# A layer step with attention, scan and ConvFFN: three value units moved between the convolved groups, two z groups behind them

## The chip, the cores and the metric

The kernel runs on one core of a Trainium2 chip. Its time is that of one execution on the device, in microseconds; what is given is the median of several executions, and beside it one execution with the hardware profiler on, from which all rows below are. TensorE does the matmuls, VectorE and GpSimd the elementwise work, ScalarE activations and copies, and SyncE's queue issues the DMAs.

## The reference

One layer on 512 prompt tokens and 32 sample tokens, with shared weights. What the change touches is the first part:

```python
h = rmsnorm(x, g_mix)
q, k, v, z, xbc, dt_raw, gates = jnp.split(h @ w_in, split_at, axis=-1)
q, k = rmsnorm(q, g_q), rmsnorm(k, g_k)             # by head
ya = band_attention(q, k, v, rel_bias)              # cached_attention for the sample tokens
xbc_c = silu(causal_dwconv(xbc, conv_ssm_w, conv_ssm_b))
xs, bm, cm = jnp.split(xbc_c, ...)                  # 32 heads, 4 groups of B and C
y, h_fin = ssd(xs, dt, a_log, bm, cm, h0)           # chunked scan
yb = rmsnorm((y + d_skip * xs) * silu(z), g_ssm)
x = x + (gate_a * (ya @ w_proj_a) + gate_b * (yb @ w_proj_b)) @ w_out
```

Then follow the ConvFFN and a gated addition. New k and v rows, the scan's state and the convolutions' last columns are outputs too.

## The kernel before, in words

All 544 tokens lie in the free dimension, features in the partitions. The large matmuls are a stream of steps (`dense_steps`, line 38), each of which makes 128 output features: 8 chunks of 6 matmuls (`mm3`, line 273: the weight as a high and a low part, the activations too, three products, two halves of 272 tokens). A step here is called a unit. The weight tile of a unit is loaded by DMA in the order of the stream, two units in one load; ScalarE rounds it to the high part (line 250), and the rest (line 254) is made by VectorE, for odd units below 40 by GpSimd. That happens one unit ahead.

A unit ends with its epilogue, which reads the two PSUM banks of `dps` (two such buffers):

- xbc units (`ep_xbc`, line 580) are the convolved ones, six to a group `proj(g)`: B, C and four x. VectorE scales them into `ext` (lines 571, 573, 574), ScalarE does the first tap (596), VectorE three more (599), ScalarE tanh (602), VectorE the product (603, 604). GpSimd copies a few columns.
- z units (`ep_z`, line 714): one VectorE scaling (717), tanh on ScalarE, two VectorE products (720, 721), a square and a sum on ScalarE and GpSimd. Four z units need the finished scan of their group.
- q and k units (`ep_qk`, line 734): scaling, square and split; nine chunks later `qk_norm` (line 745) does two small sums on TensorE, Ln and Exp on ScalarE and a product on VectorE.
- v units (`ep_v`, line 761): one VectorE scaling (763), the output DMA (764), and three chunks later five transposes on TensorE with two ScalarE copies (`v_transpose`, line 767).

TensorE's order is the order of the program's text: every matmul and transpose is pinned behind the one before (`Ordered`, line 122). Between chunks, the text from line 1136 on places other work by counts of chunks: from chunk 70 the scan, sixteen pairs of `ssd_a` (line 613) and `ssd_b` (line 664), a group of four every 65 chunks, up to chunk 330; then attention. `ssd_b` of a group's first pair, which holds stage 4 (sample tokens) and stage 0, comes at chunks 97, 162, 227 and 292. It runs the yps matmuls, adds them to xs on VectorE (line 690), and runs the st matmuls (line 696). The small PSUM tiles, `cbt`, `xst`, `yps`, `st`, `vt`, `vs`, `qn`, `cum` and others, share four banks (`sps`, line 172). `dt_sums` (line 519) comes at chunk 56.

On VectorE, ScalarE, GpSimd and SyncE the order of instructions is chosen by a list scheduler at build time, from the text's order and estimated times.

Before `do_logexp` (line 728) ScalarE's table is set for tanh and exp; `do_logexp` sets the one for Ln and Exp when the first q unit and the fourth pair's q unit come (line 1153).

Of the kernel before, what the change touches and what calls it, by code (L numbers as in the profile page):

```python
# [37 lines left out]
def dense_steps():  # L38
    def proj(g):
        return [("xbc", "B", g), ("xbc", "C", g)] + [("xbc", "x", i) for i in range(4 * g, 4 * g + 4)]  # L40

    def z(g):
        return [("z", i) for i in range(4 * g, 4 * g + 4)]

    def qkv(m):
        return [("qk", m, 0), ("qk", m, 1), ("v", m)]

    p = proj(0)
    p += proj(1) + proj(2) + z(0) + proj(3) + z(1)
    for m in range(NPAIR):  # L50
        p += qkv(m)
        if m == 2:
            p += z(2)
    p += z(3)
    p += [("ga", m) for m in range(8)]
    p += [("pa", m) for m in range(8)] + [("gb", m) for m in range(8)]
    p += [("pb", m) for m in range(8)] + [("out", m) for m in range(8)]

    def up(t):
        return [(n, i) for i in range(8 * t, 8 * t + 8) for n in ("ug", "uv")]  # L60

    def down(t):
        return [("down", t, m) for m in range(8)]

    p += up(0) + up(1) + down(0) + up(2) + down(1) + down(2)
    p += [("pw", m) for m in range(8)] + [("gate", m) for m in range(8)]
    return p
# [35 lines left out]
def unit_order():  # L103
    return [u for st in dense_steps() for u in units_of(st)]
# [12 lines left out]
def trunk(ctx: ExitStack, tc: tile.TileContext, a):  # L117
# [170 lines left out]
    class Dense:  # L288
        def __init__(self):
            self.steps = dense_steps()  # L290
            self.i = 0
            self.count = 0
            self.cur = None
            self.later = []
# [987 lines left out]
```

## Time and profile before

| | |
|---|---|
| median of 3 executions | 1355.56 us (1354.17 to 1358.21) |
| the profiled execution | 1355.77 us |
| its span, first to last instruction | 1354.1 us |
| TensorE (PE) busy | 1338.2 us |
| VectorE (DVE) busy | 852.6 us |
| ScalarE (ACT) busy | 634.4 us |
| GpSimd (POOL) busy | 313.7 us |
| TensorE's granted clock | 0.999 |

A row of instructions names the line of the kernel, the engine, the operation, the tiles written and read, and shapes; times are microseconds from the first instruction unless they are marked as ns. Idle time of an engine before an instruction is put down to what released it.

### The profile page before, as it was taken

The page shows a single profiled execution, that of the slowest core. Times are in us where ns is not written, and L with a number is a line of the kernel's source. Part 1 is how long each engine was busy: PE and PEld are TensorE (multiplying, and loading weights), DVE is VectorE, ACT ScalarE, POOL GpSimd, SP SyncE. Part 2 cuts the span into 40 slices and gives each one's busy share as a digit, 9 for nine tenths or more (in the row PEclk, how much of TensorE's full clock was granted, in tenths as well). Part 3 has the DMA queues.
Part 4 walks back from the last instruction along what each step waited for, and adds up shares of the span by engine and source line. Part 5 has one row for each costly group of instructions (what it writes and reads, how often), then busy time and mean ns, then how long its engine had stood idle before and what let it go on. Part 6 is the DMA issues. An engine that isn't in the chain of part 4 may idle for free.

```text
span 1354.1 us, 26563 instructions
## 1 busy us (share of the span) xinstructions
PE 1338.2 (99%) x11045; PEld 1307.2 (97%) x11045; DVE 852.6 (63%) x1474; ACT 634.4 (47%) x1104; POOL 313.7 (23%) x442
## 2 busy tenths in 40 slices
PE   8999999999999999999999999999999999999998
PEld 7999998999999999999999999999999999999998
DVE  7999889755775656643554335677676356753545
ACT  5465555656676667542442223534444124432342
POOL 5456365544321211100000000133332013310000
PEclk9999999999999999999999999999999999999999
DMA  5733243332533332222223422222222232222231
GB/s 182 252 100 130 83 128 121 119 132 100 177 94 114 115 111 90 67 81 94 69 89 110 143 94 73 85 94 94 94 72 85 94 111 94 76 85 94 94 107 53
DMA packets 41896, 142.15 MB, mean 105 GB/s; under 512 B 9216, under 2 KB 13232, under 8 KB 29488
## 3 DMA queue, kind: packets, MB, share of 16 engines
q1 hardware_dynamic: 41776, 140.45, 31.4%
q8 instruction: 87, 1.43, 0.4%
q14 instruction: 33, 0.27, 0.1%
HBM read 129.27 MB, written 14.31 MB: 106 GB/s over the span
## 4 chain that ended last, share of the span: by engine, by line
PE 89%; DVE 6%; ACT 2%; DMA 1%; issue 1%; SPq 0%; POOL 0%; ACTq 0%; DVEq 0%; POOLq 0%
PE dps L130 80%; PE O L130 2%; PE yps L130 2%; PE L L130 1%; PE st L130 1%; DVE cv L599 1%; DVE qs L834 1%; PE Tp L133 1%; DVE wl L254 1%; PE xst L133 0%; PE gps L130 0%; DMA wr<-in_w 0%; DVE xs L603 0%; DMA ab<-asc 0%; PE qn L130 0%
## 5 line engine op out<-in xcount | busy, mean ns | idle before, releaser
L130 PE MATMUL dps<-hi,wh 128*128 128x272 f32 x2960 | 627.0, 293 | 0.6 <-DVE ext L574 0.4
L130 PE MATMUL dps<-lo,wh 128*128 128x272 f32 x2960 | 613.1, 288 | 4.1 <-DVE lo L375 4.1
L130 PE MATMUL dps<-hi,wl 128*128 128x272 f32 x2960 | 612.1, 288 | 0.0
L130 PEld LDWEIGHTS dps<-hi,wh 128*128 128x128 f32 x2960 | 466.0, 189 | 10.5 <-issue 7.8
L130 PEld LDWEIGHTS dps<-lo,wh 128*128 128x128 f32 x2960 | 465.9, 189 | 5.0 <-DVE lo L375 5.0
L130 PEld LDWEIGHTS dps<-hi,wl 128*128 128x128 f32 x2960 | 464.9, 188 | 0.0
L250 ACT CAST wh<-wr 128x1024 fp32r<-128x1024 f32 x192 | 201.2, 1048 | 386.0 <-PE dps L130 346.6
L254 DVE TENSOR_TENSOR wl<-wr,wh 128x1024 fp32r<-128x1024 f32 x173 | 213.6, 1235 | 47.6 <-ACT wh L250 42.3
L1033 DVE SCALAR_TENSOR_TENSOR ucv<-uext,vec,ucv 128x546 f32<-128x546 f32 x96 | 75.3, 784 | 4.4 <-ACT ucv L1030 2.7
L599 DVE SCALAR_TENSOR_TENSOR cv<-ext,hv,cv 128x547 f32<-128x547 f32 x72 | 71.0, 986 | 2.1 <-ACT cv L596 1.0
L1026 POOL COPY cfo<-uext 128x2 f32<-128x2 f32 x48 | 10.4, 217 | 261.7 <-DVE uext L573 261.7
L1023 POOL MEMSET uext<- 128x2 f32 x48 | 4.5, 95 | 278.7 <-issue 278.7
L1065 DVE TENSOR_TENSOR x<-x,dps 128x544 f32<-128x544 f32 x24 | 17.3, 721 | 78.0 <-PE dps L130 78.0
L571 DVE TENSOR_TENSOR uext<-dps,rstd 128x272 f32<-128x272 f32 x48 | 21.3, 443 | 63.0 <-PE dps L130 58.3
L785 DVE CUSTOM_DVE_ANT_0 P<-L,bias 128x128 f32<-128x128 f32 (+3 forms) x64 | 30.8, 481 | 46.1 <-PE L L130 41.6
L254 POOL TENSOR_TENSOR wl<-wr,wh 128x1024 fp32r<-128x1024 f32 x19 | 48.4, 2549 | 43.9 <-ACT wh L250 42.4
L1027 POOL COPY cfo<-uext 128x2 f32<-128x2 f32 x48 | 55.5, 1157 | 0.0
L787 ACT ACTIVATE P<-P,sm 128x128 f32<-128x128 f32 (+3 forms) x64 | 36.0, 562 | 26.8 <-DVE sm L785 26.4
L660 POOL TENSOR_TENSOR ab<-ab,bc 128x512 f32<-128x512 f32 (+1 forms) x28 | 37.0, 1325 | 40.7 <-ACT ab L659 40.7
L368 ACT CAST hi<-me 128x544 fp32r<-128x544 f32 x24 | 15.5, 647 | 61.9 <-DVE me L1051 61.9
L1030 ACT ACTIVATE ucv<-uext,vec 128x546 f32<-128x546 f32 x48 | 40.7, 847 | 7.2 <-DVE uext L574 2.6
L650 ACT ACTIVATE m<-ab,tm 128x128 f32<-128x128 f32 x128 | 40.8, 389 | 6.3 <-DMA ab<-asc 6.2
(243 smaller groups left out, 1548.9 us busy)
## 6 DMA issues: line engine op xcount, KB each, us to landing
wr<-in_w SPq DMA_DIRECT2D x96, 1024.0 KB, 4.9
ab<-asc SPq DMA_DIRECT2D x32, 256.0 KB, 5.1
bsc<-evec SPq DMA_DIRECT2D x16, 320.0 KB, 8.0
bias<-bsc SPq DMA_DIRECT2D x16, 256.0 KB, 3.2
xin<-in_xT SPq DMA_DIRECT2D x8, 272.0 KB, 5.7
out_o_v<-v SPq DMA_DIRECT2D x8, 272.0 KB, 3.2
out_o_k<-qk SPq DMA_DIRECT2D x8, 272.0 KB, 2.9
x<-in_xT SPq DMA_DIRECT2D x8, 272.0 KB, 4.4
```

The costliest lines, as they stand in the source:

```text
L130: return self._pin(nc.tensor.matmul(*args, **kw))
L250: cp = S.copy(hi, r)
L254: eng.tensor_tensor(lo, r, hi.bitcast(F32), op=SUB)
L571: V.tensor_tensor(ext[:, n : n + HALF], ps[:, 0, :HALF], rstd[:, 0:HALF], op=MUL)
L599: V.scalar_tensor_tensor(y[:, :n], ext[:, j : j + n], hv[:, 24 * j + ti : 24 * j + ti + 1], y[:, :n], op0=MUL, op1=ADD)
L650: S.activation(m[:, i], ab[:Q, i], AF.Relu, scale=-1.0, bias=tm[:Q, 1, c, hd : hd + 1])
L660: G.tensor_tensor(ab, ab, cc[:, tk].unsqueeze(1).to_broadcast([128, H, Q]), op=MUL)
L785: V.tensor_tensor_reduce(out=P, in0=L, in1=B, scale=1.0, scalar=3e38, op0=ADD, op1=MIN, accum_out=nm[:n])
L787: S.activation(P, P, AF.Exp, scale=-1.0, bias=nm[:n], accum_out=sm[:n])
L1027: G.tensor_copy(cfo[:, i, 2:4], ext[:, UW - 2 : UW])
L1030: S.activation(y[:, :n], ext[:, 0:n], AF.Identity, scale=vec[:, V_FW + i : V_FW + i + 1], bias=vec[:, V_FB + i : V_FB + i + 1])
L1033: V.scalar_tensor_tensor(y[:, :n], ext[:, j : j + n], vec[:, V_FW + 48 * j + i : V_FW + 48 * j + i + 1], y[:, :n], op0=MUL, op1=ADD)
```

## The change

It reorders the units. The v units of the first three head pairs leave their places behind q and k; v of pairs 0 and 1 come behind `proj(0)`, v of pair 2 behind `proj(1)`. `z(0)` comes behind `proj(3)`, next to `z(1)`. The weights are packed in the same order, so loads and matmuls follow by themselves. In numbers of units: before, proj(0) 0 to 5, proj(1) 6 to 11, proj(2) 12 to 17, z(0) 18 to 21, proj(3) 22 to 27, z(1) 28 to 31, then q, k, v of three pairs 32 to 40; after, proj(0) 0 to 5, v 6 and 7, proj(1) 8 to 13, v 14, proj(2) 15 to 20, proj(3) 21 to 26, z(0) 27 to 30, z(1) 31 to 34, q and k of three pairs 35 to 40.

```diff
     def qkv(m):
-        return [("qk", m, 0), ("qk", m, 1), ("v", m)]
+        return [("qk", m, 0), ("qk", m, 1)] + [("v", m)] * (m >= 3)
+
+    def v(*ms):
+        return [("v", m) for m in ms]
 
     p = proj(0)
-    p += proj(1) + proj(2) + z(0) + proj(3) + z(1)
+    p += v(0, 1) + proj(1) + v(2) + proj(2) + proj(3) + z(0) + z(1)
     for m in range(NPAIR):
         p += qkv(m)
         if m == 2:
```

## Rows read from the trace of the kernel before

**Rows 1.** The page: busy time of each engine, share of the span, instructions.
```profile
PE 1338.2 (99%) x11045; PEld 1307.2 (97%) x11045; DVE 852.6 (63%) x1474; ACT 634.4 (47%) x1104; POOL 313.7 (23%) x442
```

**Rows 2.** Stages: length, busy PE, PEld, DVE, ACT, POOL, clock, DMA, GB/s.
```profile
34.00:136.00 102.00, 101.34 (x851) 97.22 (x850) 98.98 (x191) 56.88 (x106) 52.93 (x77) 1.00 0.50 162
136.00:204.00 68.00, 68.00 (x599) 63.52 (x598) 58.57 (x101) 37.56 (x79) 34.00 (x35) 1.00 0.35 107
204.00:238.00 34.00, 32.84 (x294) 30.40 (x292) 32.27 (x64) 20.35 (x42) 16.67 (x23) 1.00 0.38 116
```

**Rows 3.** Waits of PE, 28 to 345 us: total us, times, longest.
```profile
PE st L130 <- DVE xs L690: 1.8, 2, 1.2
PE dps L130 <- DVE ext L574: 0.4, 1, 0.4
PE st L130 <- DVE m L656: 0.3, 1, 0.3
```

**Rows 4.** Timeline of PE: start, length, instruction, idle time before it.
```profile
64.72 0.42 PE L130 MATMUL dps<-hi,wh 128*128 128x272 f32 x2
...
95.47 0.41 PE L130 MATMUL dps<-hi,wl 128*128 128x272 f32 x2
...
99.67 1.10 PE L130 MATMUL st<-wj,bt 128*128 128x512 f32 x2 [0.66 <-DVE xs L690]
...
164.49 2.18 PE L130 MATMUL st<-wj,bt 32*128 32x512 f32 x4
...
230.39 1.12 PE L130 MATMUL st<-wj,bt 32*128 32x512 f32 x2
232.68 1.10 PE L130 MATMUL st<-wj,bt 128*128 128x512 f32 x2 [1.16 <-DVE xs L690]
```

**Rows 5.** Timeline of DVE around the same places.
```profile
66.44 0.17 DVE L531 TENSOR_TENSOR dtt<-cum,tm 32x32 f32<-32x32 f32 x1
...
98.71 0.18 DVE L574 TENSOR_TENSOR ext<-dps,rstd 128x32 f32<-128x32 f32 x1
...
163.70 0.72 DVE L690 SCALAR_TENSOR_TENSOR xs<-xs,vec,yps 128x32 f32<-128x32 f32 x4 [0.65 <-PE yps L130]
...
227.60 2.77 DVE L599 SCALAR_TENSOR_TENSOR cv<-ext,hv,cv 128x547 f32<-128x547 f32 x1
```

**Rows 6.** Timeline of POOL: the weight split beside the last of these.
```profile
227.05 2.74 POOL L254 TENSOR_TENSOR wl<-wr,wh 128x1024 fp32r<-128x1024 f32 x1 [1.95 <-ACT wh L250]
```

**Rows 7.** DVE's busy time on tiles ext, th and v in turn, 34 to 345 us.
```profile
34.00:345.00 311.00, 87.11 (x137) 1.00 0.40 129
34.00:345.00 311.00, 25.93 (x48) 1.00 0.40 129
34.00:345.00 311.00, 2.17 (x3) 1.00 0.40 129
```

**Rows 8.** Line 599, 34 to 345 us: mean ns; then minimum, median, maximum.
```profile
L599 DVE SCALAR_TENSOR_TENSOR cv<-ext,hv,cv 128x547 f32<-128x547 f32 x69 | 68.7, 995 | 2.0 <-ACT cv L596 1.0
...
L599 DVE SCALAR_TENSOR_TENSOR cv<-ext,hv,cv x69: 767/789/2924, 35.3 to 237.7; 128x547 f32<-128x547 f32 x69
```

**Rows 9.** Timeline of ACT where z(2) begins, the table load among it.
```profile
349.13 1.28 ACT L719 ACT_TABLE_LOAD   x1
350.43 0.66 ACT L719 ACTIVATE zt<-z 128x544 f32<-128x544 f32 x1
352.64 0.66 ACT L383 ACTIVATE sq<-xs 128x544 f32<-128x544 f32 x1 [1.55 <-DVE xs L721]
```

**Rows 10.** Waits of PE, 345 us to the end.
```profile
PE L L130 <- DMA ks<-ks: 1.0, 2, 0.8
PE Ls L130 <- DVE qk L756: 0.9, 3, 0.3
PE L L130 <- ACT qs L752: 0.6, 1, 0.6
PE Tp L133 <- DVE sm L788: 0.5, 1, 0.5
```

## The prediction

> **What bounds the kernel now.** I read the page's first section before anything else: TensorE is busy for 1338 of 1354 us, VectorE for 853 [rows 1]. The change can therefore give only what TensorE still waits for, or add to it; the matmuls themselves stay, in number and in kind. Next came the stages [rows 2]. Between 34 and 136 us, where three convolved groups run in a row, VectorE is busy for 99.0 of 102 us; between 136 and 204 us, with z units beside the scan, for 58.6 of 68; between 204 and 238 us, the last convolved group, for 32.3 of 34. So VectorE is nearly full exactly where the change moves units. The question is whether TensorE feels it, and TensorE's waits answer that [rows 3]: from 28 to 345 us, all that is reordered, it waits 2.5 us in four waits. Two are st matmuls behind the VectorE operation of line 690, 1.8 us together; one is 0.3 us behind line 656; the fourth, 0.4 us, falls right behind `start`, ahead of the first moved unit, and stays.
>
> Where those two waits sit is in the timelines of TensorE, VectorE and GpSimd [rows 4 to 6]. `ssd_b` of a group's first pair (stages 4 and 0) runs two st matmuls that need PSUM banks which line 690 has to read out first. That pair comes at chunks 97, 162, 227 and 292 of the dense stream. At 97 (st at 99.67 us, 0.66 us late) and at 227 (st at 232.68 us, 1.16 us late) convolved units run beside it. At 162 the neighbours are z units, TensorE goes through its four st matmuls from 164.49 us in one piece, and VectorE stands idle for 0.65 us before line 690. In the first case VectorE is behind: TensorE has issued the last pair of a unit at 95.47 us, its evacuation ends only at 98.89 (98.71 + 0.18), and line 690 starts after that. In the second, one convolution step started at 227.60 takes 2.77 us, while GpSimd splits a weight tile from 227.05 to 229.79.
>
> **The change, part by part.** Three v units go from chunks 272 to 328 to steps 6, 7 and 14 (chunks 48 to 64 and 112 to 120); z(0) goes from chunks 144 to 176 to 216 to 248, z(1) to 248 to 280, behind the last convolved group. From step 41 on the two streams are the same. Nothing is removed: the same matmuls, transposes, copies and DMAs run, so the sum consists of waits alone.
>
> First term, the pair at chunk 97. Of a convolved unit VectorE has 87.1/23 + 25.9/24 = 4.87 us, of a v unit 2.17/3 = 0.72 us [rows 7]. Two v units just before relieve it of 2 x 4.15 = 8.3 us, more than the lag of 98.89 - 95.47 = 3.4 us. I take the wait as gone: -0.66 us; bounds -0.66 and 0.
>
> Second term, the pair at chunk 227, which now has z(0) beside it. The nearest row is the pair at 162 with z units in the old order, which waited for nothing: -1.16 us; bounds -1.16 and 0, since the tail of the last convolution (chunk 216) may still be on VectorE.
>
> Third term, the pair at chunk 162, which now stands in the middle of twelve convolved units (chunks 120 to 216). It resembles the old one at 227: five units of a group done, a GpSimd split just started. I take that price, +1.16 us; bounds 0 and +2.1, which is one convolution step held for its longest, 2.92 - 0.79 us [rows 8].
>
> Fourth, what the v units bring along. Each has five transposes (line 770 and 774), two ScalarE copies and one output DMA (line 764). The first v unit's transposes come at chunk 59, which begins at 64.72 us in the old run [rows 4], three chunks behind `dt_sums`, which takes three of the four small PSUM banks (lines 520, 537 and 541). vt takes the fourth, vs needs one back. The `cum` bank is read for the last time at 66.44 us [rows 5], so the wait has an upper end of 66.6 - 64.7 = 1.9 us; the other two banks go to ScalarE copies with no VectorE turn of their own, so I take 0. The DMA stands in SyncE's queue ahead of weight loads and of the `ab` loads and waits there for the v tile; that scaling takes 0.72 us [rows 7], against some 8 us for a unit beside the scan (the 65 chunks from one first pair to the next took 230.39 - 164.49 = 65.9 us [rows 4]). No wait in [rows 3] is on a weight load: 0, at most +0.7.
>
> Fifth, six q and k units now follow each other, and the last qk norm comes at chunk 337, one chunk behind z(2)'s first tanh at 336; in the old order it came at 329, ahead of it. The tanh loads its table at 349.13 us, 1.28 us, and runs 0.02 us later [rows 9]. Ln needs the other table, so ScalarE may have two loads more, 2.57 us. After that tanh it is idle for 1.55 us before its next instruction [rows 9], and none of TensorE's waits from there on is on a tanh [rows 10]. I take 0; bounds 0 and +2.57. The Trainium skill (ScalarE: Activation LUTs, What ACT_TABLE_LOAD costs) adds a drain of about 1.38 us to each switch, 2.66 us in all, so two would be 5.3 us by it; the row shows no such gap after the load.
>
> The sum is -0.66 - 1.16 + 1.16 = -0.7 us. The profiled execution took 1355.77 us (1354.1 of span), so it would be 1355.1; the median, 1355.56, stands 0.2 below it, hence 1354.9 us. A measurement of this kernel can tell a change of about 0.3%, 4.1 us, from none.
>
> **The rivals.** Slower: GpSimd holds up the convolution in the long run. In chunks 120 to 216 VectorE has twelve convolved units without a z unit between, some 96 x 65.9/65 = 97 us. GpSimd splits six weight tiles there (units 17 to 27, odd ones). If each one catches a convolution step at full length, it costs 6 x 2.13 = 12.8 us, of which an average of (995 - 789) ns x 3 x 12 = 7.4 us is in the old rate [rows 8]; 5.4 us are new. VectorE's idle share in the two convolved stretches is 3 to 5% [rows 2], 2.9 to 4.9 us of 97. From the point where the delays fall ahead of an evacuation or of line 690 instead of on that idle time, TensorE pays them: -0.7 + 5.4 = +4.7, 1360.3 us. For it: the row at 227.60. Against it: the old run of eighteen convolved units, nine of them beside the scan, cost TensorE 0.66 us. The Trainium skill (SBUF — State Buffer, Terms) says that of VectorE and GpSimd at their shared port pair the loser blocks for the full instruction; 2.77 against 0.79 us agrees with that.
>
> Table switches: the two loads land ahead of a softmax that TensorE's transposes wait for, +2.57 - 0.7, 1357.4 us. For it: the order of chunks 336 and 337. Against it: the idle 1.55 us.
>
> All waits go: the pair at 162 costs nothing either, and the 0.3 us behind line 656 goes; 1355.56 - 2.1 = 1353.4 us. This is also close to what a change that does nothing to TensorE would give (1355.6), and a timing alone can't part them.
>
> Faster beyond doubt: besides, the four waits of the attention stage, 1.0 + 0.9 + 0.6 + 0.5 = 3.0 us [rows 10], go because the early v units leave banks and ScalarE free; 1350.4 us. Little speaks for it: the order of steps there is unchanged, and none of these waits is on a v unit.
>
> **How the numbers follow.** Chances: the forecast 0.52, all waits go 0.14, table switches 0.12 (these three within 0.3%: 0.78), GpSimd's hold-ups 0.16 (slower), attention waits too 0.06 (faster). The range leaves out the faster rival and the end of the slower one: from 1351.8 (about all the waits gone and half of the attention's) to 1360.0 us. It is that wide upward since the bounds add up to 2.1 + 1.9 + 0.7 + 2.57 = 7.3 us, of which more than half at once is unlikely.
>
> **What would show it.** In the changed kernel the st matmuls of chunks 97 and 227 run on without a wait, the one of 162 waits about 1 us for line 690; the waits from 28 to 345 us come to 1.5 to 3 us; VectorE's busy share from 100 to 230 us is about 95%; two more table loads stand near 350 us with no TensorE wait behind them. The forecast is wrong if TensorE shows waits of dps on line 574 or 717 between 110 and 230 us (VectorE behind with evacuations), waits on vs near 65 us, waits of Ts or Tp near 356 us, or if the attention stage's waits change by over 2 us.

## The result, and the profile after

The changed kernel takes 1363.76 us in the median of six runs (1362.78 to 1367.03), the kernel before 1356.29 on the same chip (1354.17 to 1358.21). The ratio, of the means as everywhere below, is 1.0058, with a 95% interval from 1.0044 to 1.0073: slower by more than the 0.3% that can be told from no change. The forecast was 1354.9 us, and its range ended at 1360.0. The profiled execution took 1362.78 us, 7.0 more than the one of before.

The page's busy times, to set against [rows 1]: TensorE's matmuls are the same 11045 and take 3.3 us longer, VectorE works 2.6 us less, ScalarE has two instructions more.

```profile
PE 1341.5 (99%) x11045; PEld 1309.8 (96%) x11045; DVE 850.0 (62%) x1474; ACT 638.8 (47%) x1106; POOL 317.5 (23%) x442
```

The stages of [rows 2], and behind them three stretches of the place where most is lost. The columns are those of [rows 2]: length, busy PE, PEld, DVE, ACT, POOL, granted clock (TensorE's, 1.00 is 2.4 GHz and 0.50 is 1.2), DMA share, GB/s.

```profile
34.00:136.00 102.00, 100.96 (x847) 96.39 (x846) 87.81 (x171) 55.27 (x106) 45.93 (x61) 1.00 0.49 161
136.00:204.00 68.00, 68.00 (x598) 63.77 (x597) 64.89 (x119) 39.35 (x79) 38.48 (x51) 1.00 0.34 109
204.00:238.00 34.00, 31.64 (x289) 29.43 (x289) 30.44 (x57) 18.70 (x40) 15.08 (x19) 1.00 0.35 118
236.00:239.00 3.00, 1.23 (x5) 0.78 (x6) 3.00 (x7) 1.36 (x5) 2.21 (x2) 1.00 0.88 300
239.00:243.00 4.00, 4.00 (x21) 4.00 (x21) 3.99 (x9) 1.16 (x2) 1.05 (x1) 0.57 0.17 68
243.00:247.00 4.00, 4.00 (x36) 4.00 (x34) 2.69 (x4) 1.71 (x2) 0.00 (x0) 1.00 0.58 166
```

VectorE's load did move as forecast: less in the first stretch (87.8 of 102 us for 99.0), more in the second (64.9 of 68 for 58.6). In that second stretch, the middle of twelve convolved units in a row, TensorE is busy throughout. The loss stands later: from 236 to 239 us TensorE works 1.2 of 3 us, and from 239 to 243 it makes 21 matmuls where the neighbouring stretch of the same length has 36, at a mean granted clock of 0.57.

TensorE's waits, from 28 to 345 us and from there to the end, to be read beside [rows 3] and [rows 10]:

```profile
PE st L133 <- DVE xs L693: 2.4, 1, 2.4
PE vt L136 <- DVE v L766: 1.0, 2, 0.7
PE dps L133 <- DVE ext L577: 0.4, 1, 0.4
PE st L133 <- DVE m L659: 0.2, 1, 0.2
```
```profile
PE Ts L136 <- DVE Ps L792: 1.8, 1, 1.8
PE L L133 <- ACT qs L755: 1.2, 2, 0.6
PE Ls L133 <- DVE qk L759: 1.0, 3, 0.3
PE Tp L136 <- DVE sm L791: 0.5, 1, 0.5
```

The first list sums to 4.0 us where [rows 3] have 2.5; one st wait of 2.4 us stands in place of two of 1.8 together, and two vt waits are new. The second sums to 4.5 us where [rows 10] have 3.0; the Ts wait is new. That makes 1.5 + 1.5 = 3.0 us. The half clock from 239.2 to 242.6 us adds some 3.4 / 2 = 1.7. A further 1.4 us lies ahead of the first moved unit: the dps wait right behind `start` ends at 29.99 us instead of 28.56. Over the first 34 us the granted clock is 0.90 here and 0.95 before, and 0.05 x 34 = 1.7 us of full clock covers it. Over the profiles of all kernels here that point falls between 28.2 and 31.7 us, early and late in both orders, the earliest where that clock is 1.00 and the latest where it is 0.85, so one profile says nothing on it. Together 6.1 of the 7.0 us. From that point on the profiled execution is 7.0 - 1.4 = 5.6 us longer, a little below the interval of the timed difference (0.0044 x 1356.3 gives 6.0 us); the rest of that is not placed.

**The wait of 2.4 us, followed back.** Five timelines of the changed kernel between 221 and 240 us, each row with start, length, instruction and the idle time before it. TensorE first:

```profile
237.78 1.10 PE L133 MATMUL st<-wj,bt 128*128 128x512 f32 x2 [2.36 <-DVE xs L693]
```

VectorE, in the same stretch:

```profile
234.41 1.41 DVE L606 SCALAR_TENSOR_TENSOR xs<-th,cv 128x512 f32<-128x512 f32 x1 [3.42 <-ACT th L605]
235.74 1.26 DVE L607 SCALAR_TENSOR_TENSOR xs<-th,cv 128x32 f32<-128x32 f32 x1
236.92 0.71 DVE L693 SCALAR_TENSOR_TENSOR xs<-xs,vec,yps 128x32 f32<-128x32 f32 x4
```

ScalarE:

```profile
230.54 1.28 ACT L653 ACTIVATE m<-ab,tm 128x128 f32<-128x128 f32 x4 [4.70 <-DMA ab<-asc]
...
233.72 0.65 ACT L605 ACTIVATE th<-cv 128x547 f32<-128x547 f32 x1
```

SyncE's queue:

```profile
221.44 0.34 SPq L713 DMA_DIRECT2D out_o_hp<-h  x1
226.71 0.34 SPq L925 DMA_DIRECT2D out_o_cs<-cso  x1
227.14 0.86 SPq L648 DMA_DIRECT2D ab<-asc  x2
```

GpSimd:

```profile
226.02 0.66 POOL L596 COPY cso<-ext 128x3 f32<-128x3 f32 x1
```

From the top down, each engine was held by the next. The second pair of st matmuls waits for VectorE's line 693; that waits in turn behind lines 606 and 607, for which VectorE had stood idle 3.42 us; the tanh they need (line 605) is queued on ScalarE behind line 653, which waited 4.70 us for the `ab` load; that load stands in SyncE's queue behind the output DMA of the convolution's last columns (line 925), which issues nothing until GpSimd's last copies into `cso` are done, 226.7 us. SyncE's queue stood still from 221.8 to 226.7 us, 4.9 us. Lines 606 and 607 also run long here, beside GpSimd's split from 232.90 and its product from 235.22 us: 2.5 us from the start of 606 to that of 693, where the same two take 0.7 at 126.48. In the kernel before, the timeline of the same queue shows the other order:

```profile
220.25 0.86 SPq L645 DMA_DIRECT2D ab<-asc  x2
...
231.99 0.34 SPq L922 DMA_DIRECT2D out_o_cs<-cso  x1
```

In the new order the last convolved unit ends one unit earlier in the stream (chunk 216, not 224), and the list scheduler, which goes by estimated times, now puts the output DMA ahead of the two `ab` loads.

**The other two.** The vt waits are short and come from VectorE: the transposes come three chunks after the matmuls, whether the v unit's scaling (line 766) is done or not. At 66 us that scaling stands behind a weight split; at 127.19 us, for the longer wait, it stands behind the end of a convolved unit, of which two steps took 3.19 us from 122.56 on beside GpSimd. VectorE's timeline at the first place, then TensorE's at both:

```profile
64.77 1.20 DVE L257 TENSOR_TENSOR wl<-wr,wh 128x1024 fp32r<-128x1024 f32 x1
65.91 0.70 DVE L766 TENSOR_TENSOR v<-dps,rstd 128x544 f32<-128x544 f32 x1
```
```profile
66.67 0.66 PE L136 MATMUL vt<-ident,v 128*128 128x128 f32 x4 [0.33 <-DVE v L766]
...
127.96 0.66 PE L136 MATMUL vt<-ident,v 128*128 128x128 f32 x4 [0.71 <-DVE v L766]
```

And ScalarE's timeline around 355 us, to be read beside [rows 9], and behind it TensorE's instruction that waits:

```profile
353.67 1.28 ACT L722 ACT_TABLE_LOAD   x1
...
357.72 0.66 ACT L386 ACTIVATE sq<-xs 128x544 f32<-128x544 f32 x1 [2.09 <-DVE xs L724]
358.40 1.28 ACT L755 ACT_TABLE_LOAD   x1
359.69 0.87 ACT L755 ACTIVATE qs<-qn,eps 128x272 f32<-128x272 f32 x2
360.58 1.28 ACT L790 ACT_TABLE_LOAD   x1
```
```profile
363.41 0.52 PE L136 MATMUL Ts<-ident,Ps 128*128 128x128 f32 x3 [1.85 <-DVE Ps L792]
```

The last qk norm (line 755) now comes behind z(2)'s tanh (line 722): one load to go to the table of Ln, one to come back for the softmax (line 790), and the transposes of that softmax wait, one of the signs that the prediction named for being wrong.

### The profile page after: what moved, and what is told of

It is laid out like the page before. It is cut to its first block, busy times and chain, and to the rows that moved or that the text cites. A ratio compares the mean times of both kernels' runs of the same rounds, so it can differ in the third digit from the quotient of the medians.

```text
span 1361.1 us, 26563 instructions
## 1 busy us (share of the span) xinstructions
PE 1341.5 (99%) x11045; PEld 1309.8 (96%) x11045; DVE 850.0 (62%) x1474; ACT 638.8 (47%) x1106; POOL 317.5 (23%) x442
## 4 chain that ended last, share of the span: by engine, by line
PE 86%; DVE 10%; ACT 2%; issue 1%; DMA 1%; SPq 0%; POOL 0%; ACTq 0%; DVEq 0%
PE dps L133 77%; DVE cv L602 2%; PE O L133 2%; PE yps L133 2%; DVE qs L837 1%; PE L L133 1%; PE st L133 1%; PE Tp L136 1%; DVE wl L257 1%; DVE xs L606 1%; PE xst L136 0%; PE gps L133 0%; DVE m L659 0%; DVE xs L693 0%; DMA xin<-in_xT 0%
## 5 line engine op out<-in xcount | busy, mean ns | idle before, releaser
L663 POOL TENSOR_TENSOR ab<-ab,bc 128x512 f32<-128x512 f32 (+1 forms) x28 | 40.7, 1453 | 37.0 <-ACT ab L662 35.5
```

The costliest lines, as they stand in the source:

```text
L663: G.tensor_tensor(ab, ab, cc[:, tk].unsqueeze(1).to_broadcast([128, H, Q]), op=MUL)
```

## The experiments

The theory after reading the two traces: three local causes, each from moving the v units, the queue order on SyncE (the 2.4 us wait and the half clock behind it), the table of ScalarE, and v's transposes coming too soon. The rival: VectorE, with GpSimd beside it, is swamped by the long run of convolved units, and the places are only where that shows; then moving z(0) alone should be slow. Each group of experiments has its own runs of the kernel before; their medians were 1356.55, 1356.76 and 1356.48 us.

### Half of the change: the v units alone

```diff
-    p += v(0, 1) + proj(1) + v(2) + proj(2) + proj(3) + z(0) + z(1)
+    p += v(0, 1) + proj(1) + v(2) + proj(2) + z(0) + proj(3) + z(1)
```

> Only the three v units are moved; z(0) stays between proj(2) and proj(3). Theory A (separate waits, each with its own cause): the two more table loads near 355 us stay with the Ts wait of about 2.0 us, the two vt waits stay, 1.4 us together, the pair at chunk 97 is still without its 0.7 us; the pair at chunk 227 is beside convolved units as in the kernel before and waits about 1.2 us, without the 3.4 us at half clock. Time about 1356.3 + 2.0 + 1.4 - 0.7 = 1359.0 us. Theory B (the run of twelve convolved units keeps VectorE behind, and the waits seen are its consequence): the run is broken by z(0) again, so the time is back at 1356 to 1357 us.

Measured: 1360.82 us (six runs, 1358.21 to 1363.17), ratio 1.0032, 1.0020 to 1.0045. TensorE's waits from 28 to 400 us:

```profile
PE Ts L136 <- DVE Ps L792: 1.9, 1, 1.9
PE vt L136 <- DVE v L766: 1.0, 2, 0.7
PE xst L136 <- DVE m L659: 0.7, 1, 0.7
...
```

The table wait and the vt waits are there, and behind line 693 no st wait is left at chunks 97, 162 and 227; the one of 1.2 us that was expected at 227 did not come. The queue shows up as well, at another place, since the last convolved unit now ends at chunk 248: the output DMA issues at 257.92 us. ScalarE's timeline:

```profile
262.67 1.28 ACT L653 ACTIVATE m<-ab,tm 128x128 f32<-128x128 f32 x4 [4.22 <-DMA ab<-asc]
```

The next entry of the queue is the `ab` load (258.35 us). ScalarE is held there for 4.22 us, and 0.7 us of it reaches TensorE as the xst wait (read from the order of the rows, not tested). What a hold of this queue costs depends on what stands behind it at that moment.

The new waits, less the 1.8 us that went, make up about half of the 4.3 us between the medians. In the profiled execution TensorE also waits for `ks` at 493.59 and 494.70 us, 0.89 and 0.71 us, and then has a granted clock of 0.66 from 494 to 499 us, some 1.7 us lost; the order of the units there is the old one, and whether the other executions have it is not known.

### The other half: z(0) alone

```diff
-        return [("qk", m, 0), ("qk", m, 1)] + [("v", m)] * (m >= 3)
+        return [("qk", m, 0), ("qk", m, 1), ("v", m)]
...
-    p += v(0, 1) + proj(1) + v(2) + proj(2) + proj(3) + z(0) + z(1)
+    p += proj(1) + proj(2) + proj(3) + z(0) + z(1)
```

> Only z(0) is moved behind proj(3); the v units stay behind their q and k. Theory A: no further table load and no vt wait, since the last qk norm is ahead of z(2)'s first tanh again; the st wait of the pair at chunk 97 stays as before (0.7 us), the pairs at 162 and 227 cost 0 to 2.5 us more together, and a fall of the clock only if one st wait is over 2 us. Time 1356 to 1359 us. Theory B: twenty-four convolved units now stand in one run, so VectorE falls behind more than in the changed kernel: 1363 us or more.

Measured: 1355.38 us (twelve runs, 1353.88 to 1361.22), ratio 0.9994, 0.9983 to 1.0005, the same as before. Here twenty-four convolved units follow each other, twice as many as in the changed kernel, and TensorE's waits from 28 to 345 us are

```profile
PE st L130 <- DVE xs L690: 0.8, 2, 0.7
...
```

The rival falls in this form: a run of twenty-four convolved units by itself costs TensorE nothing that shows. Of the changed kernel's loss, none comes from z(0)'s new place by itself; with the v units it makes the hold of the queue hit the st matmuls of chunk 227.

### The table: the last qk norm ahead of the tanh

From the changed kernel, the norm of the last q or k unit of the third pair two chunks sooner:

```diff
-        dense.defer(6 if pools.get("ap") else 9, lambda: qk_norm(m, s, r, hi, lo, t))
+        dense.defer(6 if pools.get("ap") else 7 if (m, s) == (2, 1) else 9, lambda: qk_norm(m, s, r, hi, lo, t))
```

> The changed kernel, with the last qk norm (pair 2, k) two chunks earlier, at chunk 335, ahead of z(2)'s first tanh at 336. Theory A: the table loads at 358 and 361 us go, the Ts wait of 1.85 us falls below 0.3 us, and the time by about 2.0 us, 1363.8 to 1361.8 us. Theory B: the loads go, but TensorE's time doesn't hang on them: 1363.5 us or more. The rest of the waits, up to 345 us, stay as they are.

Measured: 1362.27 us (five runs, 1360.22 to 1363.17), ratio 1.0042, 1.0028 to 1.0055; 1.5 us less than the changed kernel. The two loads and the Ts wait are gone from its trace; the st wait (2.5 us) and the half clock remain.

### The same cost put into the kernel before

The kernel before with that norm eight chunks later, behind the tanh:

```diff
-        dense.defer(6 if pools.get("ap") else 9, lambda: qk_norm(m, s, r, hi, lo, t))
+        dense.defer(6 if pools.get("ap") else 17 if (m, s) == (2, 1) else 9, lambda: qk_norm(m, s, r, hi, lo, t))
```

> The kernel before, with the last qk norm (pair 2, k) eight chunks later, at chunk 337, behind z(2)'s first tanh at 336, and nothing else moved. Theory A: two more table loads near 350 us and a Ts wait of about 2 us, which the kernel before doesn't have: 1356.5 + 2.0 = 1358.5 us. Theory B: the loads find idle time on ScalarE and the wait doesn't appear: 1356.5 us.

Measured: 1358.20 us (eleven runs, 1357.05 to 1362.31), 1.4 above the median of its runs of before, ratio 1.0020, 1.0010 to 1.0030. The loads and the wait stand where the changed kernel has them, in the timelines of ScalarE and TensorE:

```profile
353.72 1.28 ACT L752 ACT_TABLE_LOAD   x1
...
355.90 1.28 ACT L787 ACT_TABLE_LOAD   x1
```
```profile
358.57 0.52 PE L133 MATMUL Ts<-ident,Ps 128*128 128x128 f32 x3 [1.02 <-DVE Ps L789]
```

So the table costs 1.5 us when taken from the one kernel and 1.4 when put into the other, by the medians (by the means 2.2 and 2.7), of the 2.6 us that two loads last. The second figure isn't the table's alone: the instructions stand in the same order as before up to chunk 329, and yet the st wait of 1.16 us at chunk 227 is not in this profile, where the two convolution steps ahead of it take 1.60 us and took 3.58 in the kernel before.

```profile
227.86 1.60 DVE L599 SCALAR_TENSOR_TENSOR cv<-ext,hv,cv 128x547 f32<-128x547 f32 x2
```

### The queue: the output DMA behind the last ab load

From the changed kernel; only SyncE's order differs, the data and the DMAs are the same, and in the two traces TensorE, VectorE, ScalarE and GpSimd run the same instructions in the same order:

```diff
+    ab_dma = []
...
-            nc.sync.dma_start(ab, src.unsqueeze(0).to_broadcast([128, H, Q]))
+            ab_dma.append(nc.sync.dma_start(ab, src.unsqueeze(0).to_broadcast([128, H, Q])))
...
-        nc.sync.dma_start(a["o_cs"], cso)
+        d = nc.sync.dma_start(a["o_cs"], cso)
+        tc.add_manual_dep(d.ins, ab_dma[-1].ins.name, ORDER, reason="order")
```

> The changed kernel, with one DMA moved in SyncE's queue: the output of the convolution's last columns (out_o_cs, which waits for GpSimd's last copies until 226.7 us) goes behind the scan's last ab load instead of ahead of the ab loads of 227.14 and 227.61 us. All other engines keep their order. Theory A2 (the st wait at 237.8 us comes from the queue: ab lands late, ScalarE waits 4.7 us for it with the last tanh queued behind, VectorE idles 3.4 us and reads yps late): ScalarE's wait for ab falls below 1.5 us, the st wait of 2.36 us to 0 to 1.2 us, the 3.4 us at half clock near 239 us go, and the time falls by 2.5 to 4 us, to 1360 to 1361 us. Theory B (VectorE and GpSimd are behind with the convolution): the wait stays at 2 us or more, 1363.8 us.

Measured: 1358.81 us (ten runs, 1357.78 to 1361.85), ratio 1.0022, 1.0011 to 1.0033; 5.0 us less than the changed kernel, where 2.5 to 4 were expected. Timelines of SyncE's queue, of ScalarE (the tanh) and of TensorE (the second pair of st matmuls), then the stretch from 239 to 243 us:

```profile
220.73 0.88 SPq L649 DMA_DIRECT2D ab<-asc  x2
```
```profile
230.62 0.65 ACT L605 ACTIVATE th<-cv 128x547 f32<-128x547 f32 x1
```
```profile
234.70 1.10 PE L133 MATMUL st<-wj,bt 128*128 128x512 f32 x2 [0.49 <-DVE xs L694]
```
```profile
239.00:243.00 4.00, 4.00 (x35) 4.00 (x34) 4.00 (x7) 1.98 (x3) 0.00 (x0) 1.00 0.68 170
```

The loads issue 6.4 us sooner, the tanh runs 3.1 us sooner (1.2 us of both is this profile's earlier start), the st wait shrinks from 2.36 to 0.49 us, and the clock stays at its full level: 35 matmuls in the four microseconds that had 21. Every link of the chain read above moved with the one DMA. In the two profiles TensorE gains 3.4 us at this place, as expected; the rest of the 5.0 is not placed. This is the larger part of the loss.

### Both mended

From the changed kernel, the norm two chunks sooner and the output DMA behind the last ab load:

```diff
+        dense.defer(6 if pools.get("ap") else 7 if (m, s) == (2, 1) else 9, lambda: qk_norm(m, s, r, hi, lo, t))
...
+        tc.add_manual_dep(d.ins, ab_dma[-1].ins.name, ORDER, reason="order")
```

> The same, and the last qk norm ahead of z(2)'s first tanh. Theory A: the two gains add up, since they lie 120 us apart on a path that TensorE sets: 1363.8 - 1.5 to 2.2 - 2.5 to 4 = 1358 to 1360 us, what is left over the kernel before being the two vt waits (1.4 us) and scatter of the start. Theory B: 1362 us as with the norm alone.

Measured: 1357.45 us (twelve runs, 1355.73 to 1361.45), ratio 1.0012, 1.0003 to 1.0021. The two mend 6.3 of the 7.5 us between the medians, and the norm's part beside the mended queue is 1.4 us again (1358.81 to 1357.45). What is left of TensorE's waits from 28 to 400 us, beside two short ones of 0.4 and 0.2 us, is the vt pair and less than half of the st wait that the kernel before had:

```profile
PE vt L136 <- DVE v L767: 1.0, 2, 0.7
PE st L133 <- DVE xs L694: 0.5, 1, 0.5
...
```

### The vt waits: v's transposes later

From the changed kernel, two chunks more for the first v unit, three more for the third:

```diff
-        dense.defer(3, lambda: v_transpose(m, v))
+        dense.defer({0: 5, 2: 6}.get(m, 3), lambda: v_transpose(m, v))
```

> The changed kernel, with the transposes of v 0 and v 2 five and six chunks behind their unit instead of three. Theory A: the two vt waits (0.33 and 0.7 us shown idle, 1.4 us counted on the ends of the matmuls) go, nothing else moves: 1362.4 us. Theory B: VectorE is behind there anyway, so the wait comes back at the next thing that TensorE needs from it (the scan's first stage at chunk 70, or the evacuation of the next unit): 1363.8 us.

Measured: 1367.37 us (four runs, 1365.93 to 1368.77), ratio 1.0081, 1.0068 to 1.0094; 3.6 us more than the changed kernel, which neither theory had. TensorE's waits from 28 to 345 us:

```profile
PE st L133 <- DVE xs L693: 5.0, 2, 4.7
PE st L133 <- ACT vt L775: 1.1, 1, 1.1
...
```

The vt waits are gone. In their place the copy that empties vt's bank is queued on ScalarE behind another wait for `ab` (1.81 us, line 653 at 132.53), and st matmuls wait for that bank: the copy (line 775) runs only at 133.72 us.

The st wait at chunk 227 grows to 4.7 us, and no new order is the reason: VectorE and SyncE run the same sequence as in the changed kernel, and besides the transposes only ScalarE's copies and one weight tile, its rounding and its split on GpSimd, have moved. That split now starts at 136.82 us, 2.6 us later, and beside it a convolution step on VectorE takes 2.59 us that took 0.85. VectorE is 2.0 us behind the changed kernel at 140 us, 3.6 us at 174 us, and still 3.6 us at 228: in the long run of convolved units it makes none of this up. The output DMA issues at 230.29 and `ab` at 230.72 us, and the line that the st matmuls wait for starts at 240.56 us for 236.92:

```profile
240.56 0.71 DVE L693 SCALAR_TENSOR_TENSOR xs<-xs,vec,yps 128x32 f32<-128x32 f32 x4
```

TensorE is 1.3 us behind there, so the wait should be 2.36 + 3.6 - 1.3 = 4.7 us, as it is.

The same edit in the kernel with both causes mended:

> cs_late_norm_first with the transposes of v 0 and v 2 two and three chunks later still. If the two vt waits (0.3 and 0.7 us idle, 1.4 us on the ends of the matmuls) are what is left of the change, they go and the time falls by up to 1.4 us, to 1356.1 us, no different from the kernel before. If the later transposes take banks that the scan wants next, the wait comes back there, on st of the pair near 134 us as in vt_later (1.2 us), and the time stays at 1357.5 us; the wait of 5 us near 241 us that vt_later had should be gone, since the ab loads are in front.

Measured: 1362.27 us (five runs, 1361.13 to 1362.73), ratio 1.0036, 1.0022 to 1.0049; 4.8 us more than without it. The vt waits go, by which TensorE gains 1.5 us up to 132 us, and 1.2 us for vt's bank come, as above. The st wait at chunk 227 is 2.6 us, with half clock behind it, though the queue is mended. VectorE and GpSimd are its cause, and it has the same source as in vt_later: from 174 us on VectorE runs 3.6 us behind the kernel with both causes mended, TensorE 1.3 us at most, and the line that frees the bank (694) comes 3.4 us later: 0.5 + 3.4 - 1.3 = 2.6 us. VectorE's timeline there, first with both mended, then with the transposes later:

```profile
235.01 0.71 DVE L694 SCALAR_TENSOR_TENSOR xs<-xs,vec,yps 128x32 f32<-128x32 f32 x4
```
```profile
232.27 4.66 DVE L602 SCALAR_TENSOR_TENSOR cv<-ext,hv,cv 128x547 f32<-128x547 f32 x2
...
238.37 0.71 DVE L694 SCALAR_TENSOR_TENSOR xs<-xs,vec,yps 128x32 f32<-128x32 f32 x4
```

And GpSimd's beside the two convolution steps:

```profile
232.26 2.37 POOL L257 TENSOR_TENSOR wl<-wr,wh 128x1024 fp32r<-128x1024 f32 x1 [2.07 <-ACT wh L253]
234.59 1.75 POOL L664 TENSOR_TENSOR ab<-ab,bc 128x512 f32<-128x512 f32 x1
```

The two steps take 4.66 us, where they take 1.62 from 228.66 us on with both mended, while GpSimd is idle. That coincidence adds nothing in the end: with both mended, lines 606 and 607 stand beside GpSimd instead and take 2.5 us, here 0.7. What is left is the delay of 135 to 174 us that VectorE carried through the long run. That is half of the prediction's slower rival: the run costs nothing by itself, but a delay that enters it comes out at its end.

### What the st waits are worth

All wins of the forecast were st waits. To see what they can give, two chunks of the dense stream are put between the two halves of these matmuls, and taken off the place behind, in three kernels: before, z(0) alone, and both mended.

```diff
+        if len(parts) == 2:
+            dense.run(2)
...
-        dense.run(fb)
+        dense.run(fb - 2 * (c == 1))
```

> The kernel before, with two of the dense chunks that follow a group's first ssd_b taken into it, between line 690 and the st matmuls (and two fewer behind it). If TensorE's st waits of 0.66 and 1.16 us are only a matter of VectorE being late by that much, both go and the time falls by 1.8 us to 1354.7 us. If the chunks only push the wait to the next thing (the tiles h that follow, the next stage's cbt), it stays at 1356.5 us.

Measured: 1356.08 us (eleven runs, 1354.41 to 1357.20), ratio 0.9995, 0.9986 to 1.0004. Of TensorE's waits in [rows 3] the 0.4 us behind `start` and the 0.3 us behind line 656 are left; the 1.8 us behind line 690 are gone.

The gain, 0.7 us between medians, lies within the interval. So this was the size of the prize: removing both st waits for sure is something that this measurement can hardly tell from nothing.

> Only z(0) moved, and the two dense chunks inside the first ssd_b. z_alone had st waits of 0.7 and 0.2 us left, which go here: 1355.4 - 0.9 = 1354.5 us, 0.15% below the kernel before, if the chunks push no other wait up; 1355.4 us or more if they do.

Measured: 1355.98 us (eleven runs, 1353.95 to 1357.53), ratio 0.9995, 0.9986 to 1.0003. The st waits are gone here as well, and no gain can be told.

> cs_late_norm_first with two dense chunks between line 690 and the st matmuls of each first pair. One st wait is left there, 0.5 us at 235.9 us, so the gain is 0 to 0.5 us: 1357.0 to 1357.5 us.

Measured: 1358.75 us (eleven runs, 1355.71 to 1361.85), ratio 1.0014, 1.0002 to 1.0026. The st waits are gone, and the vt waits have grown from 1.0 to 1.5 us. No order of these units tried here is faster than the kernel before by more than the measurement can tell.

## Why the prediction was wrong

**The frame held.** TensorE bounds the kernel, the matmuls stayed the same, and the time went by what TensorE waits for. But "the sum consists of waits alone" was too little: a wait can also take the clock with it, and that came to 1.7 us beside 2.4 us of waiting.

**First term, the pair at chunk 97:** right. No wait stands there in the changed kernel, nor with the v units alone.

**Second term, the pair at chunk 227:** the step that failed by most. It was priced by the pair at 162 in the old order (z units beside it, no wait, -1.16 us) with an upper end of 0; measured were +1.2 us of waiting and 1.7 of half clock, 4.1 us above the price. The likeness was of neighbours on VectorE alone. What the pair depends on besides, the `ab` load, its place in SyncE's queue and what is queued on ScalarE behind it, was not looked at. The prediction named one DMA that moves, v's own output, and left out the one that closes the convolution, `out_o_cs`, though proj(3) is its producer and was moved. With that DMA put behind the loads the wait is 0.49 us: even then the term would have been about -0.7, not -1.16.

**Third term, the pair at chunk 162:** wrong by +1.16 us. It waits for nothing in the changed kernel, and 0.2 us in the one with z(0) alone. One row of a coincidence (2.77 us at 227.60, [rows 5]) was taken for a pattern that any convolved run would show; the kernel before with the late norm, in the same order up to there, does not even have that wait.

**Fourth, what the v units bring along:** taken at 0 with an upper end of 1.9 us; measured 1.0 us of waiting. The bound held, the reason did not: the transposes waited neither for a bank nor for `cum`, but for v itself, whose scaling stood behind a split on VectorE at the first place and behind the end of a convolved unit at the second.

**Fifth, the table:** both loads came, at the place the prediction named, and were not free. The 1.55 us of idle time after the tanh [rows 9] did not cover them because that idle time lies ahead of the loads and not behind: ScalarE waits for line 724 and only then meets the norm (line 386 at 357.72 us, load at 358.40). Both loads then stand between the norm and the softmax. By the medians it cost 1.4 to 1.5 us, inside the bounds 0 and 2.57, and this was the rival "table switches" in mechanism and nearly in size. The Trainium skill (ScalarE: Activation LUTs, What ACT_TABLE_LOAD costs) would have 1.38 us of drain more for each switch; the rows show each load 0.02 us after the end of the instruction ahead of it and the next ACTIVATE 0.01 us after the load's end, so here the load's 1.28 us is the whole of it.

**The slower rival** ended near the right time (1360.3) for the wrong reason. In the changed kernel TensorE is busy for all of the 68 us from 136 to 204, and twenty-four convolved units in a row cost nothing. But the rival's second half holds: where the later transposes put a delay into the run, VectorE carried 3.6 us of delay over more than 50 us, and TensorE paid at chunk 227. And the wait of 2.36 us has some of GpSimd in it, in lines 606 and 607; how much was not tested.

**The range** was summed from bounds of 7.3 us upward and cut 4.4 us above the kernel before, on the ground that more than half at once was unlikely. The table and the vt waits came at once, each at more than half of its bound, and the largest loss, at chunk 227, was outside of all bounds: even their whole sum, 1355.6 + 7.3 = 1362.9 us, lies below the measured median.

**What stays open.** Some 1 of the 7 us in the profile, and why single runs of one kernel spread by up to 7 us; the starts alone spread by 3.5 us (28.2 to 31.7 us for the first wait behind `start`), with granted clocks of 0.85 to 1.00 over the first 34 us. What is left between the kernel with both causes mended and the kernel before, 0.7 us by the medians and 1.6 by the means, is of the order of the vt waits (1.5 us where they were taken away), but no run took these away without a new wait, so that part is argued only.

## What to carry to other kernels

When a block of work is moved, list every entry of every in-order queue that needs its results, output DMAs among them, and look at what now stands behind each: a transfer that nobody waits for can hold a load for which everything waits. A wait that is taken away is worth at most its length, here 1.8 us in all and hardly to be measured, while the delay that travelled from a DMA over ScalarE and VectorE to TensorE cost 5.0 us by the medians, so with an engine at 99% the bounds upward deserve most of the work. Idle time of an engine is a cover only if it lies between the new work and its reader; check on which side of it the new work falls. And an engine that is nearly full passes a delay on: what VectorE fell behind by between 135 and 174 us, 3.6 us, was still whole at 228.

## What the runs showed of the hardware that was not expected

- After TensorE had stood still for 2.36 us, with little work in the 3 us around it (1.2 us busy from 236 to 239), its granted clock fell to the lower of its levels, 1.2 GHz, from 239.2 to 242.6 us, while it was fully busy again; then it was back at 2.4 GHz. The kernel with the norm mended has the same (a wait of 2.5 us, a granted clock of 0.81 from 236 to 241 us and 0.84 from 241 to 246), the wait of 1.16 us at 232 us in the kernel before has not. With the v units alone it fell, to a mean of 0.66 from 494 to 499 us, behind two waits of 0.89 and 0.71 us with 0.4 us of work between them. The fall made a wait of 2.4 us cost about 4.
- A table load on ScalarE was 1.28 us and nothing more: it started 0.02 us behind the instruction ahead, and the next activation ran 0.01 us later.
- VectorE's convolution step took 0.79 us in the median [rows 8] and 2.3 us in the mean of two beside GpSimd's elementwise work on the same kind of tiles; lines 606 and 607 took 1.41 and 1.26 us in the changed kernel at 234.41 us, where the same two take 0.69 and 0.18 at 126.48.
